# Projection back of a gated feed-forward block: one group of eleven pairs by seven products each, with quarter loads and adding loads

## The chip, the cores and the metric

The kernel runs on one core of a Trainium2 chip. The metric is the device time of one execution in microseconds (us). Engines: PE (TensorE, matrix products), DVE (VectorE), ACT (ScalarE), POOL (GpSimd), SP (SyncE, which issues most transfers). PEld is PE's weight loading. A transfer issued by POOL can add to what lies at its destination; here it is called an adding load.

## What is computed

One block of a hybrid sequence model over 1024 tokens of 1024 features, all in float32: a normalised projection into two branches (a chunkwise linear recurrence and a sparse attention), a gated mix of both and an output projection, and then the part that matters here, the feed-forward block with its final norm:

```python
h = h + mixed @ w_out[l]
f = rms_norm(h, g_norm_ffn[l])
h = h + (jax.nn.silu(f @ w_gate[l]) * (f @ w_up[l])) @ w_down[l]   # D_FF = 2816
return rms_norm(h, g_final)
```

The last product, (1024 x 2816) by (2816 x 1024), is called the projection back below.

## The kernel before

Each float32 operand is split into a rounded high part and a low rest (`split_steps`, L1868: ACT copies the high part at L1865, DVE subtracts it at L1862), and a product is three matmuls, high by high, high by low and low by high (`mm3`, L352 to L355). One matmul is 128x128 by 128x512.

Large products are saved by Strassen's scheme in Winograd's form: a product of 2 by 2 blocks takes seven block products and some sums instead of eight block products. The blocks of the output are token rows by parity (r) and column halves (c); the contraction is blocked in pairs. Of the 2816 hidden features, in 22 strips of 128 (`d_gu` in HBM, one strip per t), strips 2p and 2p+1 form **pair** p.

The projection back (L2487 to L2612) takes 9 of the 11 pairs by seven products, in two groups (`GROUPS`, 4 and 5 pairs). In a group, each product q runs over the pairs with four PSUM banks (one per token block j): 12 matmuls per pair. After each product DVE adds the four banks to accumulators in SBUF (`acc`), and behind the second group `combine(q)` adds accumulators to each other, on DVE or on POOL (`BOTH`). The sums of inputs that the products need are made by DVE (`into(SUM, ...)`), eight per pair. The remaining four strips (`tl`) are multiplied plainly, each of eight row blocks by two column halves by four strips, 12 matmuls each, and behind each row block its norm follows (`square`, `rstd_steps`, `stt`) and its rows go out. Inputs come as whole strips of 512 KB (`load2`), the residual `d_h` by plain loads into the accumulators.

The stages from the output projection on are recorded as steps (`Plan.step`) and put in order by a list planner (`Plan.run`, L139) with costs for each engine and a model of when a transfer lands (`landed`, `lat`). It sets the order on every engine and leaves none to run time. Transfers by SP are modelled with a size; adding loads (`dma_add`, L1874) only had a fixed latency, and SP's model did not know of them. Adding loads are used before in three places: `wo_add` (sums of blocks of w_out), `xadd` (the input x added to the output projection) and the second half of `sums` in the feed-forward products.

Ahead of the projection back run the feed-forward products up (`product`, L2311), which write `d_gu` at the end of every second strip; before these the output projection (`wprod`, products 1, 2, 6, 5, 3, 7, 4) and the norm behind it (`stored`, `rows_f`).

```python
def mm3(ps, ah, al, bh, bl, first, last):
    nc.tensor.matmul(ps, ah, bh, start=first, stop=False)   # L353
    nc.tensor.matmul(ps, ah, bl, start=False, stop=False)   # L354
    nc.tensor.matmul(ps, al, bh, start=False, stop=last)    # L355
```

Of the kernel before, what the change touches and what calls it, by code (L numbers as in the profile page):

```python
# [8 lines left out]
F32 = mybir.dt.float32  # L9
F32R = mybir.dt.float32r  # L10
AF = mybir.ActivationFunctionType
ALU = mybir.AluOpType
# [53 lines left out]
class Plan:  # L66
# [69 lines left out]
    def run(self):  # L136
        free = self.free_banks()
        while any(self.todo.values()):
# [26 lines left out]
            if st.nd:  # L165
                st.lat = self.landed[-1] - st.end
# [6 lines left out]
def body(ctx, tc, a, out):  # L173
# [1700 lines left out]
    def dma_add(dst, src, writes, lat):  # L1874
        pl.step((("Pool", 1000.0),), lambda e: nc.gpsimd.dma_start(dst(), src(), accum_op=ALU.add), (), writes, lat=lat)
# [614 lines left out]
    RSL = (0, 1, 2, 3, 28, 29, 4, 5, 16, 17, 18, 19, 8, 9, 10, 11, 30, 12, 13, 14, 15)  # L2490
    TMP, MORE, OUT = (12, 13, 14, 15), (6, 7, 4, 5), (3, 28, 29, 16)
    cnt = {"o": 0, "r": 0, "t": 0}

    def turn(kind, ring):
        cnt[kind] += 1
        return ring[(cnt[kind] - 1) % len(ring)]

    def load2(src, reads=()):

        n = turn("r", RSL)  # L2500
        bs = pieces(n)
        dma(lambda: slot_ap(n, F32), lambda: src.rearrange("p (a c) -> p a c", a=2), reads, bs, kb=512.0)
        return bs

    def op(src, n=None):
        b = slot_buf(turn("o", OPS) if n is None else n, F32R)
        split_steps(lambda: b.ap[:, 0, :], lambda: b.ap[:, 1, :], lambda: src.ap, [src], [b], V)
        return b

    allf = list(fsb.values())  # L2510
    acc = {}
    for n, q in enumerate((1, 2, 7, 5, 6, 4, 3, 8)):
        for j in range(4):
            z = 4 * n + j
            acc[q, j] = xpiece(z - 16) if z > 15 else pl.buf((), None, allf, make=lambda z=z: big(0, F32)[:, z, :])
    pl.boost = -100
    for q, r, c in ((2, 0, 0), (4, 1, 0), (8, 1, 1), (3, 0, 1)):
        for j in range(4):
            dma(lambda q=q, j=j: acc[q, j].ap, lambda r=r, c=c, j=j: d_h[2 * j + r][:, 512 * c:512 * c + 512],
                [hdr[2 * j + r]], [acc[q, j]], kb=512.0)  # L2520

    def combine(q):

        for j in range(4):
            g = lambda n: acc[n, j]
            todo = {2: ((2, 1),), 6: ((1, 6), (7, 1), (8, 5), (8, 7), (5, 1)), 4: ((4, 7),), 3: ((3, 5),)}.get(q, ())
            for d, x in todo:
                into(BOTH, g(d), g(d), g(x), ALU.add, [g(x)])

    pl.boost = 0  # L2530
    wdn = a["w_down"]
    for gi, pairs in enumerate(GROUPS):
        ra, rb = {}, {}
        for z in range(2):
            for p in pairs:
                t = 2 * p + z
                ra[p, z] = load2(d_gu[t][:, :], [gub[t]])
                rb[p, z] = load2(wdn[P * t:P * t + P, :])
        for q in QS:
            ps = [pl.buf() for _ in range(4)]  # L2540
            for p in pairs:
                (a11, a21), (a12, a22) = ra[p, 0], ra[p, 1]
                (b11, b12), (b21, b22) = rb[p, 0], rb[p, 1]
                if q == 7:
                    s3, t3 = piece(turn("t", TMP)), piece(turn("t", TMP))
                    into(SUM, s3, a11, a21, ALU.subtract, [a11, a21])
                    into(SUM, t3, b22, b12, ALU.subtract, [b22, b12])
                    x, y = s3, t3
                elif q == 5:
                    into(SUM, a21, a21, a22, ALU.add, [a22])  # L2550
                    into(SUM, b12, b12, b11, ALU.subtract, [b11])
                    x, y = a21, b12
                elif q == 6:
                    into(SUM, a11, a21, a11, ALU.subtract, [a21])
                    into(SUM, b11, b22, b12, ALU.subtract, [b22, b12])
                    x, y = a11, b11
                elif q == 4:
                    into(SUM, b21, b21, b11, ALU.subtract, [b11])
                    x, y = a22, b21
                elif q == 3:  # L2560
                    into(SUM, a12, a12, a11, ALU.subtract, [a11])
                    x, y = a12, b22
                else:
                    x, y = (a11, b11) if q == 1 else (a12, b21)
                oa, ob = op(x), op(y)

                def go(e, oa=oa, ob=ob, ps=ps, first=p == pairs[0], last=p == pairs[-1]):
                    for j in range(4):
                        js = slice(P * j, P * j + P)
                        mm3(ps[j].ap, oa.ap[:, 0, js], oa.ap[:, 1, js], ob.ap[:, 0, :], ob.ap[:, 1, :], first, last)  # L2570
                pl.step((("PE", 12 * 226.7),), go, [oa, ob], ps)
# [92 lines left out]
```

## Time and profile before

| | us |
|---|---|
| median of 3 runs | 1555.11 (1553.91 to 1556.33) |
| the profiled execution, device time | 1554.78 |
| its span, first to last instruction | 1553.0 |
| around the span | 1.8 |
| mean granted clock | 0.997 |

The span is that of one execution; the sum below is made against it, and the median of the runs lies 0.33 us above the profiled execution's own time. Times in rows count from the span's start. In a row of a timeline the first number is the start, the second the length, then engine, line, operation, out<-in, shapes and count, and in brackets how long the engine had been idle before and what ended that. Matmuls overlap: the row of one reads 0.39 us, while the next starts 0.23 us after it.

### The profile page before, as it was taken

Reading aid. Unit: us, or ns where it says so; the run is one execution under the profiler, and the core shown is the slowest. Engines: PE = TensorE matmul, PEld = TensorE weight load, DVE = VectorE, ACT = ScalarE, POOL = GpSimd, SP = SyncE. Lnnn points to the kernel's source line nnn. Section 1 sums busy time; section 2 is a strip of 40 time slices with the busy share of each in tenths; the row PEclk is TensorE's granted clock in tenths of the full one; section 3 lists DMA queues with packets and bytes.
Section 4 is the critical chain, followed back from the end, with each engine's and each line's share of the span. In section 5 each row is a group of like instructions: output and inputs, shape, how many; then the busy total and the mean of one; then the engine's idle time right before and its main releaser. Section 6 shows DMA issues by size and latency. Waiting matters only on the chain.

```text
span 1553.0 us, 22069 instructions
## 1 busy us (share of the span) xinstructions
PE 1516.0 (98%) x7642; PEld 1277.9 (82%) x7642; DVE 1174.5 (76%) x2464; ACT 803.4 (52%) x1708; POOL 194.4 (13%) x252
## 2 busy tenths in 40 slices
PE   6999999999999999999999999999999999999997
PEld 5877888887989888888887878888888888788876
DVE  6978888875988687865676795666666666988996
ACT  5325565653878688875434663333333333454433
POOL 2000000013121322110001510000000000001140
PEclk9999999999999999999999999999999999999999
DMA  8424755589242914239917825444454445560302
GB/s 276 121 76 127 232 162 170 162 239 269 42 114 40 186 39 115 48 81 345 259 41 176 177 75 129 110 110 113 117 168 109 109 109 183 190 217 1 109 1 108
DMA packets 185959, 211.84 MB, mean 136 GB/s; under 512 B 10536, under 2 KB 143046, under 8 KB 185848
## 3 DMA queue, kind: packets, MB, share of 16 engines
q1 hardware_dynamic: 153848, 179.91, 36.9%
q0 software_dynamic: 31712, 29.87, 12.8%
q8 instruction: 60, 0.98, 0.3%
q10 hardware_dynamic: 288, 0.66, 0.1%
q14 instruction: 51, 0.42, 0.1%
HBM read 159.97 MB, written 58.29 MB: 141 GB/s over the span
## 4 chain that ended last, share of the span: by engine, by line
PE 85%; DVE 6%; DMA 5%; ACT 2%; issue 1%; SPq 0%; POOL 0%; DVEq 0%; ACTq 0%; POOLq 0%
PE PS L354 16%; PE PS L355 16%; PE PS L353 16%; PE bk L353 5%; PE bk L354 5%; PE bk L355 5%; PE T L1526 4%; PE obank L1548 2%; PE obank L1546 2%; PE d L353 2%; PE d L355 2%; PE d L354 2%; DMA UTL_float<-in_x 1%; DMA rp<-in_w_in 1%; DMA d_mg<-S 1%
## 5 line engine op out<-in xcount | busy, mean ns | idle before, releaser
L1862 DVE TENSOR_TENSOR UTL_float<-PS,UTL_float 128x512 f32<-128x512 f32 x144 | 97.3, 689 | 80.2 <-PE PS L355 79.2
L1535 DVE TENSOR_TENSOR TL<-T,TH 128x512 fp32r<-128x512 f32 (+1 forms) x184 | 103.4, 582 | 28.7 <-ACT TH L1531 27.8
L1531 ACT ACTIVATE TH<-T 128x512 fp32r<-128x512 f32 (+1 forms) x184 | 90.3, 510 | 26.3 <-PE T L1526 23.1
L354 PE MATMUL PS<-quad_float32r,sl_float32r 128*128 128x512 f32 x240 | 93.4, 389 | 0.0
L353 PE MATMUL bk<-UTH,op 128*128 128x512 f32 x192 | 77.4, 403 | 0.0
L353 PE MATMUL PS<-quad_float32r 128*128 128x512 f32 x196 | 76.3, 389 | 0.0
L355 PE MATMUL PS<-quad_float32r 128*128 128x512 f32 x196 | 76.3, 389 | 0.0
L354 PE MATMUL PS<-quad_float32r 128*128 128x512 f32 x196 | 76.3, 389 | 0.0
L355 PE MATMUL bk<-UTH,op 128*128 128x512 f32 x192 | 75.0, 391 | 0.0
L354 PE MATMUL bk<-UTL,op 128*128 128x512 f32 x192 | 74.9, 390 | 0.0
L354 PE MATMUL PS<-quad_float32r,whi 128*128 128x512 f32 x176 | 68.6, 390 | 0.7 <-DVE quad_float32r L1862 0.7
L354 PE MATMUL PS<-quad_float32r,wh 128*128 128x512 f32 x164 | 63.8, 389 | 0.0
L353 PE MATMUL bk<-T,op 128*128 128x512 f32 x144 | 58.1, 404 | 0.0
L355 PE MATMUL bk<-T,op 128*128 128x512 f32 x144 | 56.3, 391 | 0.0
L354 PE MATMUL bk<-T,op 128*128 128x512 f32 x144 | 56.2, 390 | 0.0
L353 PE MATMUL d<-UTH,whi 128*128 128x512 f32 x128 | 53.1, 414 | 1.7 <-ACT mg L1398 1.5
L1865 ACT ACTIVATE quad_float32r<-quad_float 128x512 fp32r<-128x512 f32 x57 | 32.8, 622 | 41.3 <-PE PS L354 29.4
L1560 POOL DMA_DIRECT2D d_yn<-os x32 | 31.9, 996 | 173.9 <-DMA d_yn<-os 40.7
L354 PEld LDWEIGHTS PS<-quad_float32r,sl_float32r 128*128 128x128 f32 x240 | 45.1, 188 | 9.3
L355 PE MATMUL d<-UTH,wlo 128*128 128x512 f32 x128 | 50.4, 394 | 0.0
L354 PE MATMUL d<-UTL,whi 128*128 128x512 f32 x128 | 50.4, 393 | 0.0
L353 PE MATMUL PS<-UTH_float32r,sl_float32r 128*128 128x512 f32 x124 | 48.4, 390 | 0.0
(1488 smaller groups left out, 4933.9 us busy)
## 6 DMA issues: line engine op xcount, KB each, us to landing
rp<-in_w_in SPq DMA_DIRECT2D x22, 512.0 KB, 4.8
d_gu<-UTL_float SPq DMA_DIRECT2D x44, 256.0 KB, 3.2
sl_float<-in_w_up SPq DMA_DIRECT2D x20, 512.0 KB, 3.8
quad_float<-d_mg SPq DMA_DIRECT2D x32, 256.0 KB, 7.2
d_rep<-d_row SPq DMA_DIRECT2D x8, 960.0 KB, 7.4
quad_float<-d_gu SPq DMA_DIRECT2D x12, 512.0 KB, 6.1
quad_float<-in_w_down SPq DMA_DIRECT2D x12, 512.0 KB, 6.5
raw<-in_w_gate SPq DMA_DIRECT2D x11, 512.0 KB, 4.2
```

The costliest lines, as they stand in the source:

```text
L353: nc.tensor.matmul(ps, ah, bh, start=first, stop=False)
L354: nc.tensor.matmul(ps, ah, bl, start=False, stop=False)
L355: nc.tensor.matmul(ps, al, bh, start=False, stop=last)
L1526: nc.tensor.transpose(pt[:, z, P * r:P * r + P], e, ident)
L1531: nc.scalar.activation(hl[0][:, 0:m], pt[:, 0:m], AF.Copy)
L1535: nc.vector.tensor_tensor(hl[1][:, 0:m], pt[:, 0:m], cast32(hl[0])[:, 0:m], ALU.subtract)
L1546: nc.tensor.matmul(po, vv, th[:, z, :], start=(st[1] == 0), stop=False)
L1548: nc.tensor.matmul(po, vv, tl[:, z, :], start=False, stop=(st[1] == st[2]))
L1560: low_half.append(lambda: nc.gpsimd.dma_start(dst, half(1), accum_op=ALU.add))
L1862: return pl.step(alts, lambda e: ENG[e].tensor_tensor(out_(), x(), y(), alu), reads, writes, **kw)
L1865: return pl.step((("ACT", cost),), lambda e: nc.scalar.activation(out_(), x(), fn), reads, writes, **kw)
```

## The change

The projection back becomes one group of all 11 pairs by seven products. The four strips that were multiplied plainly are gone. Inputs are loaded by quarters of a pair (128x512, 256 KB; `load`, `gu`, `wd`). Of the sums of inputs, those of `w_down` are made by adding loads on POOL (`more`), those of `d_gu` by DVE, four per pair (`into(V, a3...)` and three `neg_sum`). A product ends in four banks that are copied by ACT or combined by DVE into four blocks of four pieces (`v1`, `v7`, `w4`, `c22`); `acc` and `combine` are gone. The residual is added by 16 adding loads from `d_h`. In the last product the first six pairs run over all four token blocks, the last five block by block, and each block's norm follows it. The ring of split operands (`OPS`) grows from 12 to 14 slots, seven pairs. In the final norm, the first column half of seven of the eight row blocks is scaled by ACT and multiplied by the gain on POOL (the `two` form of `stt`); before this was so for both halves of one row block.

The planner now knows the size of adding loads and lets them and SP's transfers share one model of landing. With this it also orders a few steps of the output projection and the feed-forward products differently.

```diff
-                st.lat = self.landed[-1] - st.end
+                st.lat = max(st.lat, self.landed[-1] - st.end)
...
-    def dma_add(dst, src, writes, lat):
-        pl.step((("Pool", 1000.0),), lambda e: nc.gpsimd.dma_start(dst(), src(), accum_op=ALU.add), (), writes, lat=lat)
+    def dma_add(dst, src, writes, lat, reads=(), kb=256.0):
+        pl.step((("Pool", 1000.0),), lambda e: nc.gpsimd.dma_start(dst(), src(), accum_op=ALU.add), reads, writes, lat=lat, kb=kb, nd=1)
...
-        dma_add(lambda: b.ap, lambda: wo_blk(kh, ch), [b], 12000.0)
+        dma_add(lambda: b.ap, lambda: wo_blk(kh, ch), [b], 12000.0, kb=1024.0)
...
-    GROUPS = ((0, 1, 2, 3), (4, 5, 6, 7, 8))
-    QS = (1, 2, 7, 5, 6, 4, 3)
-    OPS = (20, 21, 22, 23, 24, 25, 26, 27, 31, 33, 32, 34)
...
-    tl = range(2 * (GROUPS[-1][-1] + 1), NFF)
...
+    NPR = NFF // 2
+    OPS = (20, 21, 22, 23, 24, 25, 26, 27, 31, 33, 32, 34, 6, 7)
+    cnt = [0]
+    allf = list(fsb.values())
+    room = [(n, z) for n in (0, 1, 2, 3, 28, 29, 4, 5, 30, 8, 9, 10, 11, 16, 17, 18, 19, 14, 15, 12, 13) for z in range(2)]
+    room += [("u", n) for n in range(16)]
...
+    def more(b, src, reads=()):
+        dma_add(lambda: b.ap, lambda: src, [b], 5500.0, reads)
+
+    def mult(ps, js, ops, first, last):
+        def go(e):
+            for j in js:
+                for n, (oa, ob) in enumerate(ops):
+                    cs = slice(P * j, P * j + P)
+                    mm3(ps[j].ap, oa.ap[:, 0, cs], oa.ap[:, 1, cs], ob.ap[:, 0, :], ob.ap[:, 1, :], first and n == 0, last and n == len(ops) - 1)
+        pl.step((("PE", 3 * 226.7 * len(js) * len(ops)),), go, [b for o in ops for b in o], [ps[j] for j in js])
+
+    def product(xs, ys):
+        ps = [pl.buf() for _ in range(4)]
+        for p in range(NPR):
+            mult(ps, range(4), [(op(xs[p]), op(ys[p]))], p == 0, p == NPR - 1)
+        return ps
...
+    for p in PR:
+        a1[p] = gu(0, 0, p)
+        xx[p] = load(wd(0, 0, p))
+    ps = product(a1, xx)
+    for j in J:
+        act(587.0, at(v1[j]), at(ps[j]), AF.Copy, [ps[j]], [v1[j]])
+    a3, yy = {}, {}
+    for p in PR:
+        a3[p] = gu(0, 1, p)
+        yy[p] = load(wd(0, 1, p))
+        more(yy[p], wd(1, 1, p))
+        more(xx[p], wd(0, 1, p))
+        into(V, a3[p], a1[p], a3[p], ALU.subtract, [a1[p]])
+    ps = product(a3, yy)
...
+    for p in PR:
+        a4[p] = gu(1, 1, p)
+        neg_sum(a3[p], a3[p], a4[p])
+        neg_sum(a1[p], a3[p], a1[p])
+    ps = product(a1, xx)
+    for j in J:
+        into(V, w4[j], ps[j], v1[j], ALU.add, [ps[j], v1[j]])
+    give(*a1.values())
+    for p in PR:
+        more(xx[p], wd(1, 1, p))
+    ps = product(a3, xx)
+    for j in J:
+        neg_sum(w4[j], ps[j], w4[j])
+        into(V, c22[j], w4[j], v7[j], ALU.subtract, [w4[j], v7[j]])
+        into(V, v7[j], ps[j], v7[j], ALU.add, [ps[j]])
+        into(V, v7[j], v7[j], v1[j], ALU.add, [v1[j]])
+    for p in PR:
+        more(xx[p], wd(1, 0, p))
+    ps = product(a4, xx)
...
+    for r, c, b in ((1, 0, v7), (1, 1, c22), (0, 0, v1), (0, 1, w4)):
+        for j in J:
+            more(b[j], *row(r, c, j))
...
+    ps = product(a2, zz)
+    give(*zz.values())
+    normal(1, (0, 1), (v7, c22))
+    normal(1, (2, 3), (v7, c22))
...
+    for p in range(6):
+        mult(ps, J, [(op(a2[p]), op(bb[p]))], p == 0, False)
+    tail = [(op(a2[p]), op(bb[p])) for p in range(6, NPR)]
+    for j in J:
+        mult(ps, [j], tail, False, True)
+        into(V, w4[j], w4[j], ps[j], ALU.subtract, [ps[j]])
+        square(at(w4[j]), 2 * j, 1, [w4[j]])
+        normal(0, (j,), (v1, w4))
```

Three places of the order of instructions. The first is ACT in the output projection, where product 5's operands are split (`sl_5` and `sl_7` are its left operand's high parts, `sl_14` and `sl_12` its right operand's; `sq,sml` is the sum of squares of a row block that waits for an adding load of x). This is one piece of the difference:

```order
 L1865 ACTIVATE wl_7547<-ra_7544 128x512
-L2097 ACTIVATE sq,sml<-UTL_float_8419 128x512
 L1865 ACTIVATE sl_5_float32r<-UTH_float_7797 128x512 x2
 L1865 ACTIVATE sl_7_float32r<-UTH_float_7797 128x512 x2
 L2097 ACTIVATE sq,sml<-UTL_float_8419 128x512
-L1865 ACTIVATE sl_14_float32r<-quad_2_float_7569 128x512 x2
-L1865 ACTIVATE sl_12_float32r<-quad_2_float_7569 128x512
+L1865 ACTIVATE sl_14_float32r<-quad_2_float_7569 128x512
 L2097 ACTIVATE sq,sml<-UTL_float_8419 128x512
```

The left operand's four splits now stand ahead of the first sum of squares and no longer wait for its load; the right operand's still stand behind it.

The second is DVE at the end of the second group before, behind product 4 (`UTH` and `UTL` are accumulators; `whi`, `wlo`, `wh`, `wl` are the split operands of product 3's first pairs):

```order
L1862 TENSOR_TENSOR UTL_float_8419<-UTL_float_8419,PS 128x512 x4
L1862 TENSOR_TENSOR UTH_float_11728<-UTH_float_11728 128x512
L1862 TENSOR_TENSOR UTH_float_11728<-UTH_float_11728,UTL_float_8419 128x512
L1862 TENSOR_TENSOR UTL_float_8419<-UTL_float_8419,UTH_float_11728 128x512
L1862 TENSOR_TENSOR UTH_float_11728<-UTH_float_11728 128x512 x2
L1862 TENSOR_TENSOR UTL_float_8419<-UTL_float_8419,UTH_float_11728 128x512 x2
L1862 TENSOR_TENSOR whi_7018<-ra_7544,whi_7018 128x512
L1862 TENSOR_TENSOR wlo_7019<-sl_20_float_9298,wlo_7019 128x512
```

and what stands in its place now, behind the fourth product (`UTL` holds the pieces v1, v7, w4, c22; `quad_20` on the left and `sl` are operands of the fifth product's later pairs):

```order
L2039 SCALAR_TENSOR_TENSOR UTL_float_8419<-PS,UTL_float_8419 128x512 x2
L1862 TENSOR_TENSOR UTL_float_8419<-UTL_float_8419 128x512 x2
L1862 TENSOR_TENSOR UTL_float_8419<-PS,UTL_float_8419 128x512 x2
...
L1862 TENSOR_TENSOR quad_20_float32r<-UTH_float_11928,quad_20_float32r 128x512
L1862 TENSOR_TENSOR quad_20_float32r<-sl_20_float_9298,quad_20_float32r 128x512
```

The 16 sums behind the fourth product stand in one block, ahead of the splits of the fifth product's later pairs; the sums of accumulators that stood ahead of product 3's first pairs are gone.

The third is POOL from the last feed-forward weight on. Before:

```order
L1875 DMA UTL_float_8419<-in_w_up 128x4x128
L1862 TENSOR_TENSOR UTH_float_11728<-UTH_float_11728 128x512 x3
L1862 TENSOR_TENSOR UTL_float_8419<-UTL_float_8419,UTH_float_11728 128x512 x3
L1862 TENSOR_TENSOR UTH_float_11728<-UTH_float_11728,UTL_float_8419 128x512 x2
...
L1862 TENSOR_TENSOR sl_20_float_9072<-sl_20_float_9072,sl_20_float_9068 128x512 x2
```

Now (60 adding loads and seven multiplications; `sl`, `raw`, `ra` at the start are the w_down quarters `xx`, `quad_20_float_11632` and `11701` the quarters `yy`; `d_h` is the residual):

```order
L1875 DMA sl_20_float_8957<-in_w_down 128x512
L1875 DMA quad_20_float_11632<-in_w_down 128x512
L1875 DMA sl_20_float_9000<-in_w_down 128x512
L1875 DMA quad_20_float_11632<-in_w_down 128x512
L1875 DMA sl_20_float_9068<-in_w_down 128x512
L1875 DMA sl_20_float_9072<-in_w_down 128x512
L1875 DMA quad_20_float_11701<-in_w_down 128x512
...
L1875 DMA UTL_float_8419<-d_h_152 128x512
...
L1862 TENSOR_TENSOR UTH_float_11928<-UTH_float_11928 128x512 x3
```

The 20 additions of accumulators are gone from POOL; each adding load of an `xx` stands in a queue with those of `yy`, in the order of the pairs.

## Rows read from the trace of the kernel before

**Rows 1.** The page, part 1 (busy time, share of the span, instructions) and the first line of part 4 (the chain that ended last, by engine).

```profile
PE 1516.0 (98%) x7642; PEld 1277.9 (82%) x7642; DVE 1174.5 (76%) x2464; ACT 803.4 (52%) x1708; POOL 194.4 (13%) x252
...
PE 85%; DVE 6%; DMA 5%; ACT 2%; issue 1%; SPq 0%; POOL 0%; DVEq 0%; ACTq 0%; POOLq 0%
```

**Rows 2.** Timeline of PE in the projection back: its first matmul (1324.88), the 61st matmul (1338.48) and the one behind it, the first two matmuls of product 3 of the second group, the end of the slow stretch behind them, and the last matmul.

```profile
1324.88 0.39 PE L353 MATMUL PS<-quad_float32r 128*128 128x512 f32 x1
...
1338.48 0.40 PE L353 MATMUL PS<-wl,wh 128*128 128x512 f32 x1
1339.81 0.50 PE L354 MATMUL PS<-wl,wh 128*128 128x512 f32 x1 [0.94 <-DVE wl L1862]
...
1483.92 0.39 PE L353 MATMUL PS<-wlo,whi 128*128 128x512 f32 x1
1486.42 0.80 PE L354 MATMUL PS<-wlo,whi 128*128 128x512 f32 x1 [2.12 <-DVE wlo L1862]
...
1490.11 0.39 PE L354 MATMUL PS<-wlo,whi 128*128 128x512 f32 x1
...
1544.76 0.39 PE L355 MATMUL PS<-quad_float32r,sl_float32r 128*128 128x512 f32 x1
```

**Rows 3.** Busy time by stretch: stretch, its length, busy us (and instructions) of PE, PEld, DVE, ACT, POOL, granted clock of PE, busy share of the DMA engines, GB/s. The first is in the output projection, the others in the projection back.

```profile
840.00:860.00 20.00, 18.34 (x79) 14.28 (x78) 19.07 (x32) 17.27 (x36) 4.81 (x5) 1.00 0.60 130
...
1324.88:1340.00 15.12, 14.18 (x63) 11.45 (x62) 12.02 (x20) 9.52 (x18) 0.00 (x0) 1.00 1.03 395
1340.00:1483.00 143.00, 143.00 (x631) 118.35 (x631) 133.43 (x203) 67.40 (x117) 19.46 (x13) 1.00 0.26 92
1480.00:1490.00 10.00, 7.88 (x29) 6.07 (x28) 10.00 (x13) 3.02 (x6) 4.46 (x3) 0.83 0.00 0
1490.00:1545.00 55.00, 55.00 (x244) 45.30 (x242) 45.35 (x104) 20.88 (x51) 9.82 (x8) 1.00 0.16 58
```

**Rows 4.** Timeline of DVE ahead of the two waits of PE (rows 2): the split that ended the first, and the sums and splits ahead of the second.

```profile
1339.08 0.68 DVE L1862 TENSOR_TENSOR wl<-quad_float,wl 128x512 fp32r<-128x512 f32 x1
...
1478.31 3.48 DVE L1862 TENSOR_TENSOR UTH_float<-UTH_float 128x512 f32<-128x512 f32 x2
1481.70 3.46 DVE L1862 TENSOR_TENSOR UTL_float<-UTL_float,UTH_float 128x512 f32<-128x512 f32 x2
1485.09 0.68 DVE L1862 TENSOR_TENSOR whi<-ra,whi 128x512 fp32r<-128x512 f32 x1
1485.69 0.68 DVE L1862 TENSOR_TENSOR wlo<-sl_float,wlo 128x512 fp32r<-128x512 f32 x1
...
1488.10 3.08 DVE L1862 TENSOR_TENSOR quad_float32r<-quad_float,quad_float32r 128x512 fp32r<-128x512 f32 x5
```

**Rows 5.** Timeline of POOL in the same stretch: the additions of accumulators.

```profile
1479.50 1.73 POOL L1862 TENSOR_TENSOR UTH_float<-UTH_float,UTL_float 128x512 f32<-128x512 f32 x1
1481.31 1.62 POOL L1862 TENSOR_TENSOR UTH_float<-UTH_float 128x512 f32<-128x512 f32 x1
1483.01 1.61 POOL L1862 TENSOR_TENSOR UTL_float<-UTL_float,UTH_float 128x512 f32<-128x512 f32 x1
```

**Rows 6.** Timeline of ACT in the output projection: the sum of squares that waits for an adding load of x, and the splits of product 5's operands behind it.

```profile
839.55 0.63 ACT L2097 ACTIVATE sq<-UTL_float 128x512 bf16<-128x512 f32 x1 [6.86 <-DMA UTL_float<-in_x]
...
840.19 2.18 ACT L1865 ACTIVATE sl_float32r<-UTH_float 128x512 fp32r<-128x512 f32 x4
...
842.88 1.65 ACT L1865 ACTIVATE sl_float32r<-quad_float 128x512 fp32r<-128x512 f32 x3
```

**Rows 7.** Timeline of PE there: the first matmuls of product 5.

```profile
843.55 0.50 PE L353 MATMUL PS<-sl_float32r,sl_float32r 128*128 128x512 f32 x1 [0.98 <-ACT sl_float32r L1865]
844.59 0.50 PE L354 MATMUL PS<-sl_float32r,sl_float32r 128*128 128x512 f32 x1 [0.54 <-DVE sl_float32r L1862]
```

**Rows 8.** The line of the adding loads: their length on POOL (min/median/max ns) for a piece of 128x512, and the time from issue to landing of all its adding loads.

```profile
L1875 POOL DMA_DIRECT2D UTL_float<-in_x x16: 850/867/1421, 824.6 to 868.6; - x16
...
DMA to landing us min/median/max: 4.0/6.9/17.0
```

**Rows 9.** Timeline of POOL in the output projection: two adding loads issued back to back.

```profile
865.69 1.82 POOL L1875 DMA_DIRECT2D UTL_float<-in_x  x2 [0.90 <-DVE UTL_float L1862]
```

**Rows 10.** Timeline of DVE in the same two microseconds: subtractions with both inputs in SBUF.

```profile
865.31 1.89 DVE L1862 TENSOR_TENSOR quad_float32r<-quad_float,quad_float32r 128x512 fp32r<-128x512 f32 x3
```

**Rows 11.** DMA queue of the adding loads in the stretch 700 to 900 us: packets, MB, share of that stretch's 200 us of 16 engines.

```profile
q0 software_dynamic: 4944, 9.44, 26.7%
```

**Rows 12.** DMA issues from 1300 us on: out<-in, count, KB each, median us from issue to landing.

```profile
quad_float<-d_gu SPq DMA_DIRECT2D x12, 512.0 KB, 6.1
...
d_gu<-UTL_float SPq DMA_DIRECT2D x4, 256.0 KB, 7.2
```

**Rows 13.** Timeline of SP: the write of the next-to-last piece of `d_gu`.

```profile
1326.81 0.32 SPq L1872 DMA_DIRECT2D d_gu<-UTL_float  x1
```

**Rows 14.** Timeline of DVE behind the last matmul: the last sum, and the last scaling.

```profile
1545.26 0.69 DVE L1862 TENSOR_TENSOR UTL_float<-UTL_float,PS 128x512 f32<-128x512 f32 x1 [1.82 <-PE PS L355]
...
1549.05 0.74 DVE L2127 SCALAR_TENSOR_TENSOR raw<-UTL_float,sml,sl_float 128x512 f32<-128x512 f32 x1
```

More of the change, by code (lines that the diff above doesn't have):

```diff
@@ L2505, in op, with take @@
[L2505 to L2506 removed]
+    NPR = NFF // 2
[4 more added lines that the diff above has]
+    room += [("u", n) for n in range(16)]
+    def take():
+        h = room.pop(0)
+        b = pl.buf([("V", h[1])], None, allf, make=lambda: big(0, F32)[:, h[1], :]) if h[0] == "u" else fpiece(*h)
+        b.home = h
+        return b
@@ L2507, in op, with give, load @@
+    def give(*bs):
+        for b in bs:
+            room.append(b.home)
+    def load(src, reads=()):
+        b = take()
+        dma(lambda: b.ap, lambda: src, reads, [b])
+        return b
+    def op(src):
+        b = slot_buf(OPS[cnt[0] % len(OPS)], F32R)
+        cnt[0] += 1
         split_steps(lambda: b.ap[:, 0, :], lambda: b.ap[:, 1, :], lambda: src.ap, [src], [b], V)
         return b
[L2510 to L2515, printed above, removed]
@@ L2530, in body @@
-    pl.boost = 0
-    wdn = a["w_down"]
[L2532 to L2571, printed above, removed]
-            for j in range(4):
-                d = acc[q, j]
-                if gi == 0 and q not in (2, 3, 4):
-                    act(480.0, lambda d=d: d.ap, lambda s=ps[j]: s.ap, AF.Copy, [ps[j]], [d])
-                else:
-                    ew(V, lambda d=d: d.ap, lambda d=d: d.ap, lambda s=ps[j]: s.ap, ALU.add, [ps[j]], [d])
-            if gi == len(GROUPS) - 1:
-                combine(q)
@@ new lines, in normal @@
+                dma(lambda i=i, c=c: out[P * i:P * i + P, 512 * c:512 * c + 512], lambda o=o: o.ap, [o])
+                give(o)
+    J = range(4)
+    PR = range(NPR)
+    v1, v7, w4, c22 = ([xpiece(4 * n + j) for j in J] for n in range(4))
+    at = lambda b: (lambda: b.ap)
+    a1, xx = {}, {}
+    for p in PR:
[5 more added lines that the diff above has]
+    a3, yy = {}, {}
@@ new lines, in body @@
+    for r, c, b in ((1, 0, v7), (1, 1, c22), (0, 0, v1), (0, 1, w4)):
+        for j in J:
+            more(b[j], *row(r, c, j))
+    gl = [load(a["g_final"][512 * c:512 * c + 512].partition_broadcast(P)) for c in range(2)]
+    for j in J:
+        square(at(c22[j]), 2 * j + 1, 1, [c22[j]])
+        into(V, v7[j], ps[j], v7[j], ALU.add, [ps[j]])
+        square(at(v7[j]), 2 * j + 1, 0, [v7[j]])
+    a2, zz = {}, {}
+    for p in PR:
+        a2[p] = gu(1, 0, p)
+        zz[p] = load(wd(1, 0, p))
@@ new lines, in body @@
+    ps = product(a2, zz)
+    give(*zz.values())
+    normal(1, (0, 1), (v7, c22))
+    normal(1, (2, 3), (v7, c22))
+    for j in J:
+        into(V, v1[j], ps[j], v1[j], ALU.add, [ps[j]])
+        square(at(v1[j]), 2 * j, 0, [v1[j]])
+    bb = {}
+    for p in PR:
+        bb[p] = load(wd(1, 1, p))
+        neg_sum(a2[p], a3[p], a2[p])
+    ps = [pl.buf() for _ in J]
+    for p in range(6):
+        mult(ps, J, [(op(a2[p]), op(bb[p]))], p == 0, False)
+    tail = [(op(a2[p]), op(bb[p])) for p in range(6, NPR)]
```

69 lines of the change are left out of this document (21 added, 48 removed).

## Prediction, made before the changed kernel ran

> **What bounds the kernel now.** I read the page's shares first: PE is busy 98% of the span and carries 85% of the chain that ended last, while DVE is at 76% [rows 1]. So what the change is worth is read on PE: how many matmuls it issues, and where it waits. The timeline of PE gives both for the projection back, which begins at 1324.88 and issues its last matmul at 1544.76 [rows 2]. From 1324.88 to 1338.48 there are 60 steps, so a step is 13.60 / 60 = 0.2267 us. The code counts 948 matmuls: 7 products x 9 pairs x 12 = 756, and 16 blocks x 12 = 192. At 0.2267 that is 214.9 us; the stretch takes 1544.76 + 0.23 - 1324.88 = 220.1. PE thus loses 5.2 us here, and the timeline shows where. One wait at 1339.81: the step from 1338.48 is 1.33 us instead of 0.23, 1.1 lost. One at 1486.42: 2.50 instead of 0.23, 2.27 lost, and behind it nine steps to 1490.11 take 3.69 us instead of 2.04, 1.65 lost; the stretch by time shows a granted clock of 0.83 there [rows 3]. Together 5.0 of the 5.2.
>
> Both waits end on a DVE split. The stretches show why: from 1340 to 1483 DVE is busy 133.4 of 143 us [rows 3], and ahead of the second wait four sums of accumulators take 1.7 us each (3.48 and 3.46 for two) where five splits in a row take 3.08, that is 0.6 each [rows 4]. In the same microseconds POOL adds accumulators [rows 5].
>
> **The change, part by part.**
>
> *Matmuls.* 7 x 11 x 12 = 924, 24 fewer. PE has no other work there, so each is worth a step: 24 x 0.2267 = **-5.4 us**.
>
> *DVE's load.* A split or sum costs 0.6 [rows 4]. Before, seven products of nine pairs have 126 splits of the low part and 72 sums of inputs, then 16 splits, 56 sums out of PSUM (40 on DVE here, 16 on ACT), 32 sums of accumulators shared with POOL, and 16 last sums. Now: 154 splits, 44 sums of inputs, 32 sums at the ends of products. By product, in a window of 11 x 12 x 0.2267 = 29.9 us, DVE has 33 operations in the second (20 us), 22 + 22 in the third (26.6), 22 + 4 in the fourth, 22 + 16 in the fifth (23), and under 27 us in each of the last two, norms included. None fills its window, and the ring lets splits run up to seven pairs, 19 us, ahead. The two places that cost PE time, the first sums of product 7 beside its splits and the sums of accumulators beside POOL, are gone. I take both waits and the slow steps behind the second as gone: **-5.0 us**; the bounds are 0 (a wait of equal size elsewhere) and -5.2.
>
> *The 16 sums behind the fourth product* stand in front of later splits on DVE. They take 16 x 0.6 to 0.7, some 10 us from the first finished bank, about 2 us before the product's end. The split of the fifth product's seventh pair behind them is then done about 10 us after that end, and needed 6 x 2.72 = 16.3 us after it. Cover 6 us, cost 0.
>
> *POOL's queue.* An adding load of this size occupies POOL for 0.87 us and lands after 6.9 (4.0 to 17.0) [rows 8]. Each `xx` quarter is read by one product's split and needed by the next product's: one window, 29.9 us, later. The load needs at most 0.9 + 17.0 + 1.2 for the new split, so 10 us are left. Eleven issues take 10 us of a window. Cost 0, but this is the part with the least room (first rival).
>
> *SP's queue.* The last pair's `d_gu` quarter can be read back only when its strip is written. That write goes out at 1326.81 [rows 13] and takes 7.2, the load some 6.1 [rows 12], both splits 1.3: 1341.4; PE wants it at 1324.88 + 10 x 2.72 = 1352.1. Queued behind it on SP are the second product's quarters from the sixth pair on: the sixth is loaded by about 1341, has its adding load by 1351 and its splits by 1353, and is due at 1354.8 + 13.6 = 1368.4. Cost 0.
>
> *Output projection.* There ACT waited 6.86 us for an adding load of x in front of a sum of squares, with eight splits of product 5 queued behind [rows 6]; PE then waited 0.98 and 0.54 on these splits [rows 7], 1.66 us idle in that stretch [rows 3]. Now four of the splits stand ahead of that wait and the rest between sums of squares. The right operand's first high part would be out at about 840.8 instead of 843.4. Bounds: 0 (the later sums wait as long) and -1.7; I take **-1.2**, nearer the full size, since PE needs the first half of the splits first.
>
> *POOL's seven multiplications* of the final norm. The trace prices them: a DVE sum of two SBUF inputs beside POOL's additions took 1.7 instead of 0.6 [rows 4, 5], so each costs DVE up to 1.1 us. Four run in the last two products' windows, 4.4 us that fit; three near the end beside sums that read PSUM, like the sum of 0.69 at the end [rows 14]. The Trainium skill, page "SBUF — State Buffer", section "Who interferes with whom", says that a DVE instruction with two SBUF inputs contends with a GpSimd instruction that reads SBUF, and not with one that only writes it. The trace agrees with the first half (1.7 us against 0.6); by the second half the adding loads would cost DVE nothing.
>
> *Tail.* From the last sum to the span's end: 1553.0 - 1545.26 = 7.7 us [rows 14]. The last block's chain is the same (sum, square, norm, two scalings on DVE, two stores). Cost 0; 0.5 either way.
>
> **Sum.** 1554.78 - 5.4 - 5.0 - 1.2 = 1543.2 for the profiled execution; the median of the runs lies 0.33 above it: **1543.5 us**.
>
> **Rivals.**
>
> *1. Adding loads fill the DMA engines.* In 700 to 900 us their queue took 26.7% of 200 us for 9.44 MB [rows 11], 5.7 us per MB; plain loads run at 395 GB/s when full [rows 3], 2.5 us per MB. Until the second product's end (1385), from about 1308 on, 36 quarters (9.4 MB, 24 us) and 22 adding loads (5.8 MB, 33 us) must pass: 57 of 72 us to the last split. If adding loads run half as slow again, 73 us, and the second product's last pairs come some 2 us late, then the same once more in the third: 4 to 6 us, as large as the waits that went. 1548.5. For it: the DMA share was 1.03 in the first stretch [rows 3]. Against it: that was 512 KB loads in a burst, and the first pairs' quarters are now fetched long before.
>
> *2. Slower: POOL's issues hold DVE up.* If an adding load's issue blocked DVE as POOL's additions do (1.1 us each), then the second product's window would hold 20 + 22 x 1.1 = 44 us of DVE work in 29.9, the third 26.6 + 12 = 39, the fifth 23 + 16 x 1.1 = 41: 34 us too much, 1577. The point from which it eats the whole gain of 11.6 is 0.65 us per issue (49 issues, less the 20 us of room in these three windows). Against it: beside two issues of POOL three DVE subtractions took 1.89 us, 0.6 each [rows 9, 10].
>
> *3. POOL's issues wait for DVE.* Where DVE leaves a tenth of the time, as in the third window (26.6 of 29.9), an issue that could only run in DVE's pauses would take 0.87 / 0.11 = 8 us, eleven of them 87 us instead of 29.9, and PE would wait near 57 us: 1600. Against it: the two issues beside a full DVE took 1.82 us, 0.9 each [rows 9, 10]. The Trainium skill has such a rule on the page "SBUF — State Buffer", section "SBUF: two separate sides": a DMA from the GpSimd queue starves for descriptors while DVE runs in a 2-port mode. By that rule this change would lose; the trace shows no such wait with these float32 sums.
>
> *4. No change.* The waits move (rival 1 in full, some 5 us), the output projection gains nothing, and the last block by block stretch leaves DVE late by its norm chain of 3.4 to 3.9 us per block where PE takes 15 x 0.2267 = 3.4: up to 3 us at the end. 1543.5 + 5 + 1.2 + 3 = 1552.7.
>
> **Chances.** The forecast (1541 to 1546) 0.72; rival 1 (1546 to 1551) 0.17; rival 4 0.05; rival 2 0.04; rival 3 0.02. A difference under 0.2%, 3.1 us, can't be told from none. So faster 0.72 + 0.17 = 0.89, same 0.05, slower 0.06. The range for 8 in 10 runs from 1540.5 (all bounds at their good end, and half a microsecond of the tail) to 1549.5 (well into rival 1).
>
> **What would show it.** Right: 24 fewer matmuls; PE from the first to the last matmul of the projection back in about 209.5 us with steps of 0.2267 and a granted clock of 1.00; no wait of PE on a split; DVE under 0.9 busy; POOL's issues 0.87 each and DVE's splits 0.6 beside them; product 5 of the output projection with less than 0.5 us of wait. Wrong: waits of PE at the start of the second or third product with DVE waiting for a transfer (rival 1), DVE operations over 1 us beside issues (rival 2), issues over 1 us (rival 3), or a last sum later than 0.5 us behind the last matmul (rival 4).

## The result, and the profile after

| | before | after |
|---|---|---|
| median of the runs compared | 1554.51 (4 runs, 1553.69 to 1556.33) | 1544.32 (4 runs, 1542.82 to 1546.87) |
| the profiled execution / its span | 1554.78 / 1553.0 | 1544.09 / 1542.3 |

The changed kernel takes 0.9935 of the time before (95% interval 0.9917 to 0.9952): about 10 us faster, beyond the 0.2% that can be told from none. The median lies 0.8 us above the forecast. Where the 10.7 us between the two spans went is read on PE.

The page after, part 1 and the first line of part 4 [rows 1]:

```profile
PE 1507.2 (98%) x7618; PEld 1271.8 (82%) x7618; DVE 1130.6 (73%) x2393; ACT 807.6 (52%) x1715; POOL 225.0 (15%) x297
...
PE 85%; DVE 6%; DMA 6%; ACT 2%; issue 1%; SPq 0%; DVEq 0%; ACTq 0%; POOLq 0%
```

24 matmuls fewer are listed. Timeline of PE: the first matmul of product 5 of the output projection and the one wait left there [rows 7], then the first and the last matmul of the projection back [rows 2]:

```profile
842.36 0.39 PE L353 MATMUL PS<-sl_float32r,sl_float32r 128*128 128x512 f32 x1
...
844.30 0.50 PE L354 MATMUL PS<-sl_float32r,sl_float32r 128*128 128x512 f32 x1 [0.17 <-DVE sl_float32r L1862]
...
1323.54 0.39 PE L353 MATMUL PS<-quad_float32r 128*128 128x512 f32 x1
...
1532.75 0.39 PE L355 MATMUL PS<-sl_float32r,sl_float32r 128*128 128x512 f32 x1
```

From 1323.54 to 1532.75 + 0.23 are 209.44 us, which is 924 x 0.22667: no wait and no slow step is left in this stage. Before it was 220.1, so 10.7 went here. The stage also begins 1.34 earlier. What lies behind the last matmul grew: 1542.3 - 1532.98 = 9.3, where it was 1553.0 - 1544.99 = 8.0. Sum: -10.7 - 1.3 + 1.3 = -10.7.

The stretches of the projection back after, columns as in [rows 3]:

```profile
1323.54:1355.00 31.46, 31.46 (x140) 26.08 (x139) 21.36 (x34) 14.66 (x25) 11.49 (x14) 1.00 1.10 273
1355.00:1385.00 30.00, 30.00 (x134) 24.82 (x134) 26.41 (x44) 15.74 (x28) 5.00 (x6) 1.00 0.97 306
1385.00:1415.00 30.00, 30.00 (x134) 24.86 (x133) 18.79 (x31) 12.92 (x23) 12.04 (x14) 1.00 0.99 208
...
1475.00:1505.00 30.00, 30.00 (x134) 24.86 (x133) 28.04 (x51) 19.25 (x38) 6.51 (x4) 1.00 0.19 71
```

PE fills every stretch at a granted clock of 1.00. The DMA engines are full or nearly so for 90 us (the last two columns: their share, 0.97 to 1.10, and GB/s). Their transfers from 1326 to 1345, by queue and by issue:

```profile
q0 software_dynamic: 1160, 2.11, 60.2%
q1 hardware_dynamic: 1801, 3.28, 49.6%
...
quad_float<-d_gu SPq DMA_DIRECT2D x6, 256.0 KB, 15.6
quad_float<-in_w_down POOLq DMA_DIRECT2D x6, 256.0 KB, 14.3
```

The adding loads (q0) hold the engines 0.602 x 19 / 2.11 = 5.4 us per MB, the plain ones 2.9, and a quarter lands 15.6 us after its issue where `d_gu` took 6.1 [rows 12]. Yet PE waits for none.

Behind the fourth product, DVE's block of sums and POOL's adding loads beside it:

```profile
1442.35 1.28 DVE L2039 SCALAR_TENSOR_TENSOR UTL_float<-PS,UTL_float 128x512 f32<-128x512 f32 x2
1443.55 1.28 DVE L1862 TENSOR_TENSOR UTL_float<-UTL_float 128x512 f32<-128x512 f32 x2
...
1450.75 1.28 DVE L1862 TENSOR_TENSOR UTL_float<-UTL_float 128x512 f32<-128x512 f32 x2
1451.95 0.68 DVE L1862 TENSOR_TENSOR quad_float32r<-UTH_float,quad_float32r 128x512 fp32r<-128x512 f32 x1
```

```profile
1444.53 7.07 POOL L1875 DMA_DIRECT2D UTL_float<-d_h  x8 [17.26 <-DVE UTL_float L1862]
```

Sums with two SBUF inputs keep to 0.6 us beside eight issues of 0.88; beside POOL's additions they took 1.7 [rows 4, 5]. At the end, DVE and POOL behind the last products:

```profile
1530.39 0.74 DVE L2127 SCALAR_TENSOR_TENSOR quad_float<-UTL_float,sml,UTH_float 128x512 f32<-128x512 f32 x1
1531.32 0.98 DVE L2106 TENSOR_TENSOR sml<-sml 128x1 f32<-128x1 f32 x1 [0.19 <-ACT sq L2097]
...
1533.61 0.69 DVE L1862 TENSOR_TENSOR UTL_float<-UTL_float,PS 128x512 f32<-128x512 f32 x1
...
1535.14 0.95 DVE L2106 TENSOR_TENSOR sml<-sml 128x1 f32<-128x1 f32 x1 [0.19 <-ACT sq L2097]
1536.13 0.15 DVE L2107 TENSOR_SCALAR sml<-sml 128x1 f32<-128x1 f32 x1
```

```profile
1526.91 1.29 POOL L1862 TENSOR_TENSOR sl_float<-sl_float,UTH_float 128x512 f32<-128x512 f32 x1 [34.50 <-ACT sl_float L2123]
1530.69 1.59 POOL L1862 TENSOR_TENSOR quad_float<-quad_float,UTH_float 128x512 f32<-128x512 f32 x1 [2.49 <-ACT quad_float L2123]
1534.52 1.56 POOL L1862 TENSOR_TENSOR quad_float<-quad_float,UTH_float 128x512 f32<-128x512 f32 x1 [2.24 <-ACT quad_float L2123]
```

The norm's first tiny sum, 128x1, takes 0.98 and 0.95 us where its neighbours take 0.15, and it ends when POOL's multiplication ends: 1532.30 and 1532.28, 1536.09 and 1536.08. The other way round, DVE's scaling of 1530.39, which also has two SBUF inputs but started before POOL's multiplication, keeps the 0.74 of [rows 14], and that multiplication takes 1.59 where the one of 1526.91 took 1.29. The first of the two slow sums also makes the last sum of a product late: that starts 0.63 behind the last matmul's end, not the 0.27 of [rows 2, 14].

### The profile page after: what moved, and what is told of

The parts are those of the page before. It is cut to its first block, busy times and chain, and to the rows that moved or that the text cites. A ratio compares the mean times of both kernels' runs of the same rounds, so it can differ in the third digit from the quotient of the medians.

```text
span 1542.3 us, 22142 instructions
## 1 busy us (share of the span) xinstructions
PE 1507.2 (98%) x7618; PEld 1271.8 (82%) x7618; DVE 1130.6 (73%) x2393; ACT 807.6 (52%) x1715; POOL 225.0 (15%) x297
## 4 chain that ended last, share of the span: by engine, by line
PE 85%; DVE 6%; DMA 6%; ACT 2%; issue 1%; SPq 0%; DVEq 0%; ACTq 0%; POOLq 0%
PE PS L354 16%; PE PS L353 16%; PE PS L355 16%; PE bk L353 5%; PE bk L354 5%; PE bk L355 5%; PE T L1526 4%; PE obank L1548 2%; PE obank L1546 2%; PE d L353 2%; PE d L355 2%; PE d L354 2%; DMA UTL_float<-in_x 1%; DMA d_mg<-S 1%; DMA ra<-in_w_gate 1%
## 5 line engine op out<-in xcount | busy, mean ns | idle before, releaser
L1862 DVE TENSOR_TENSOR UTL_float<-PS,UTL_float 128x512 f32<-128x512 f32 x160 | 107.5, 688 | 85.2 <-PE PS L355 84.1
L354 PE MATMUL PS<-quad_float32r,sl_float32r 128*128 128x512 f32 x216 | 84.0, 389 | 0.0
L353 PE MATMUL PS<-quad_float32r 128*128 128x512 f32 x192 | 74.8, 390 | 0.0
L355 PE MATMUL PS<-quad_float32r 128*128 128x512 f32 x192 | 74.7, 389 | 0.0
L354 PE MATMUL PS<-quad_float32r 128*128 128x512 f32 x192 | 74.7, 389 | 0.0
L354 PE MATMUL PS<-quad_float32r,whi 128*128 128x512 f32 x168 | 65.5, 390 | 0.7 <-DVE quad_float32r L1862 0.7
L353 PE MATMUL PS<-UTH_float32r,sl_float32r 128*128 128x512 f32 x124 | 48.4, 391 | 0.0
L355 PE MATMUL PS<-UTH_float32r,sl_float32r 128*128 128x512 f32 x124 | 48.3, 389 | 0.0
L725 ACT ACTIVATE op<-S 128x512 fp32r<-128x512 f32 x40 | 25.1, 629 | 43.6 <-PE bk L354 35.0
```

The source lines that it names most:

```text
L725: step1("ACT", 525.0, lambda: nc.scalar.activation(h, src(), AF.Copy), [r], [b])
L1862: return pl.step(alts, lambda e: ENG[e].tensor_tensor(out_(), x(), y(), alu), reads, writes, **kw)
```

## Experiments

They ran on three chips, each beside the kernel before. "Stage" is from the first to the last matmul of the projection back, "end" what lies behind it, both of the profiled execution.

**The changed kernel again.**

> The changed kernel unchanged, as the measure for the other runs of this chip. Theory and rivals alike: 1544.3 us within 1.5, and the same stretches as in its first profile: from the first to the last matmul of the projection back 209.4 us, behind the last matmul 9.3.

Measured: 1545.3 us, 0.9933 of before (0.9919 to 0.9947); stage 209.44, end 9.3. But the stage began at 1324.72, 1.2 us later than in the first profile. What delayed it stands ahead of the feed-forward products, on PE:

```profile
893.34 0.72 PE L353 MATMUL PS<-UTH_float32r,whi 128*128 128x512 f32 x1 [1.11 <-ACT UTH_float32r L1865]
894.55 0.79 PE L354 MATMUL PS<-quad_float32r,whi 128*128 128x512 f32 x1 [0.49 <-DVE quad_float32r L1862]
895.14 0.63 PE L355 MATMUL PS<-UTH_float32r,whi 128*128 128x512 f32 x1
```

Behind three short waits, eleven matmuls go at a granted clock of 0.50 (the stretch from 895 to 899), which is 1.2 of 2.4 GHz: 0.43 us from one to the next, against 0.23, 2.2 us in all; this execution had reached the place 1.3 us earlier than the first profile (893.34 instead of 894.61). Over all 14 profiled executions here there were no such steps at this place in four and 5 to 11 in ten, with the old and with the new order, and the stage began between 1322.3 and 1325.9.

**Only the planner's model, in the kernel before, and the changed kernel without it.** In the first the transfer model alone is new:

```diff
-                st.lat = self.landed[-1] - st.end
+                st.lat = max(st.lat, self.landed[-1] - st.end)
...
+        pl.step(..., reads, writes, lat=lat, kb=kb, nd=1)
```

> The kernel before with the planner's new landing model of adding loads alone; the projection back is the old one. Theory (the output projection's gain of 1.3 us comes from this model alone, through the new order of ACT): PE's waits of 0.98 and 0.54 us at the start of product 5 go, the projection back starts near 1323.5 instead of 1324.9, and the time is 1.3 us less than that of the kernel before, about 1553.2. Rival (the gain belongs to something else in the change): the waits stay and the time is that of the kernel before within 0.3 us in the place where the projection back starts.

Measured: 0.9994 of before (0.9984 to 1.0003), 1554.62 us. Both waits went: product 5 began at 842.34 without one. The stage began at 1324.26, 0.6 earlier, since seven slow steps gave back 1.4.

In the second, `nd=1` is kept for the adding loads of the projection back alone:

> The changed kernel with the planner's old model for the three old uses of adding loads; the new projection back keeps the new model. Theory: the output projection takes its old order again, product 5 waits some 1.5 us again, the projection back starts near 1324.9 and then runs its 209.4 us without a wait; 1.3 us more than the changed kernel, about 1545.6. Rival: no place where PE waits comes back, 1544.3; or the projection back gains waits too because its start is ordered differently, 1547 or more.

Measured: 1545.71 us, 0.9938 of before (0.9926 to 0.9951), beside 0.9933 of the changed kernel. The waits came back, 1.09 and 0.54; the stage began at 1324.53 and took 209.44. So the model moves the splits and takes the two waits away, as forecast, and in the old projection back it gives nothing more (the stage took 220.2). What it does for the order of the new projection back was not tested, since this run keeps it there. Its worth in the whole time isn't resolved: the half clock behind it takes some or all of it in part of the executions. The stage began at 1325.1 in the mean of the three profiled executions with the old order, at 1324.0 in that of the eleven with the new one, and single executions of either differ by more than that.

**The norm's tiny sum with one input as a scalar operand.**

```diff
+            if len(rows) == 1:
+                nc.vector.tensor_scalar(at(2), at(0), at(1), 1.0 / D, ALU.add, ALU.mult)
+                nc.vector.tensor_scalar(at(2), at(2), 1.0, EPS, ALU.mult, ALU.add)
+                return
```

> The changed kernel with the tiny sum of the final norm (128x1, two inputs in SBUF) written as a tensor_scalar with one input as a scalar operand, wherever a norm covers one row block. Theory (the two tiny sums at the end take 0.95 and 0.98 us instead of 0.16 because they read two SBUF inputs while POOL multiplies): they take 0.2 each, the end behind the last matmul becomes 8.0 to 8.5 us instead of 9.3, and the time about 1543.4. Rival 1 (the scalar operand contends with POOL as well): 0.9 us each again, 1544.3. Rival 2 (the end is set by the last sum, which starts late, or by the store, not by the tiny sum): the sum gets short and the end stays at 9.3.

Measured: 1543.73 us, 0.9929 of before (0.9917 to 0.9942). On DVE:

```profile
1532.22 0.21 DVE L2107 TENSOR_SCALAR sml<-sml 128x1 f32<-128x1 f32 x1 [0.19 <-ACT sq L2097]
...
1533.97 0.69 DVE L1862 TENSOR_TENSOR UTL_float<-UTL_float,PS 128x512 f32<-128x512 f32 x1
...
1535.51 0.21 DVE L2107 TENSOR_SCALAR sml<-sml 128x1 f32<-128x1 f32 x1 [0.19 <-ACT sq L2097]
```

0.21 instead of 0.95, both in the midst of a POOL multiplication (1531.60 to 1533.18 and 1534.66 to 1536.44), the last sum 0.19 behind the last matmul's end (1533.78), the end 8.1 instead of 9.3. The trace shows the 1.2 us at their place; between whole runs they lie inside the intervals.

**The last three multiplications on DVE instead of POOL.**

```diff
-... c == 0 and i != 6)
+... c == 0 and r == 1)
```

> The changed kernel with the last product's three multiplications on DVE instead of POOL. Theory (POOL's three multiplications cost the end 0.8 us through the tiny sum that they slow, but save DVE three scalings of 0.67): the tiny sums take 0.16 us again, DVE's last sum starts right behind the last matmul, but two scalings of the block before now stand ahead of the last norm; the end is 9.3 to 9.8 us, the time as the changed kernel's or 0.4 us more. Rival (POOL's multiplications are a loss as a whole): the end falls to 8.0 to 8.5, the time by about 1 us.

Measured: 1545.52 us, 0.9942 (0.9927 to 0.9957); tiny sums of 0.16, the end 9.5. Giving POOL the multiplications is neither a gain nor a loss; what cost was the form of the sum beside them.

**The kernel before with all sums of accumulators on DVE.**

```diff
-                into(BOTH, g(d), g(d), g(x), ALU.add, [g(x)])
+                into(V, g(d), g(d), g(x), ALU.add, [g(x)])
```

> The kernel before with the 32 sums of accumulators all on DVE, none on POOL. Theory (POOL's additions beside DVE's, which took 1.7 us each instead of 0.6, made the second wait): behind product 4 of the second group 16 sums of 0.6, 9.6 us, stand where 7 sums took 11.6; its split is done some 1.4 us earlier, the wait of 2.27 us at 1486 falls to about 1, the slow clock behind it may go, and the time is 1.4 to 3.9 us under the kernel before, 1551.5 to 1554. Rival (DVE has too much to do there, whatever POOL does): 20 more sums are 12 us more for DVE in two products, PE waits at other splits, and the time is that of before or up to 3 us more, 1555 to 1558.

Measured: 1.0006 of before (0.9997 to 1.0014). The sums took 0.6 each, the first split behind them came at 1483.05 instead of 1485.09, and PE still waited, twice, without slow steps:

```profile
1484.39 0.50 PE L354 MATMUL PS<-quad_float32r 128*128 128x512 f32 x1 [1.81 <-DVE quad_float32r L1862]
1494.01 0.50 PE L355 MATMUL PS<-quad_float32r 128*128 128x512 f32 x1 [0.94 <-DVE quad_float32r L1862]
```

The stage took 219.5 instead of 220.1. The theory falls: POOL's contention cost DVE about what POOL took off it. The sums were enough for a wait by themselves. They stand behind product 6 and not, as the orders ahead of the prediction have it, behind product 4. In the kernel before, DVE adds product 6's banks, then the sums of accumulators follow, and product 4's banks come only behind them:

```profile
1471.07 2.47 DVE L1862 TENSOR_TENSOR UTL_float<-UTL_float,PS 128x512 f32<-128x512 f32 x4
1473.46 1.53 DVE L1862 TENSOR_TENSOR UTH_float<-UTH_float 128x512 f32<-128x512 f32 x1
...
1491.11 2.46 DVE L1862 TENSOR_TENSOR UTL_float<-UTL_float,PS 128x512 f32<-128x512 f32 x4
```

**The changed kernel with 16 sums more behind its fourth product.**

```diff
+        for alu in (ALU.add, ALU.subtract) * 2:
+            into(V, w4[j], w4[j], v1[j], alu, [v1[j], ps[j]])
         neg_sum(w4[j], ps[j], w4[j])
```

> The changed kernel with 16 sums more on DVE behind the fourth product (each w4 block has v1 added and subtracted twice; nothing else changes but rounding). No additions on POOL stand beside them. Theory (the old second wait was the amount of DVE work behind a product, and the cover there is now some 6.3 us: the split behind the block is done at 1453.2 and its pair due at 1459.5): 9.6 us more eat the cover, PE waits 3.0 to 3.6 us in the fifth product, slow clock for up to 1.7 us more; 1547 to 1550. Rival (DVE's work alone makes no wait, it needed POOL beside it): no wait, 1544 to 1545.

Measured: 1551.09 us, 0.9962 of before (0.995 to 0.9974). DVE's block ran from 1443.90 to 1463.12 at 0.6 a sum, and PE:

```profile
1464.47 0.79 PE L354 MATMUL PS<-quad_float32r 128*128 128x512 f32 x1 [3.00 <-DVE quad_float32r L1862]
1465.06 0.63 PE L355 MATMUL PS<-quad_float32r 128*128 128x512 f32 x1
```

```profile
1465.00:1470.00 5.00, 5.00 (x13) 3.87 (x12) 5.00 (x10) 1.97 (x6) 2.67 (x4) 0.50 1.12 226
```

A wait of 3.0 and 13 slow steps behind it, at a granted clock of 0.50 (the stretch from 1465): the stage took 215.6, 6.1 more. DVE's sums alone bring such a wait back, of the size that the cover of 6.3 us says (9.6 - 6.3 = 3.3). The time lies above the 1550 that I had allowed, mainly because the slow steps cost 2.6 us, not 1.7. One of the six executions took 1546.75.

**The w_down sums on DVE, by plain loads, instead of adding loads.**

```diff
     def more(b, src, reads=()):
-        dma_add(lambda: b.ap, lambda: src, [b], 5500.0, reads)
+        if reads:
+            dma_add(lambda: b.ap, lambda: src, [b], 5500.0, reads)
+            return
+        t = load(src)
+        into(V, b, b, t, ALU.add, [t])
+        give(t)
```

> The changed kernel with the w_down sums made by plain loads and additions on DVE instead of adding loads (the residual is still added by adding loads). Theory (the adding loads are what keeps DVE under its window): the second product has 33 + 22 operations of 0.6 us on DVE, 33 us in 29.9, the third 44 + 11, also 33 where it was 26.6; with seven pairs of lead some of it is caught, PE waits 3 to 8 us there in sum, 1548 to 1553. Rival (the ring's lead of 19 us takes all of it, and the adding loads were not needed): no wait, 1545.

Measured: 1543.6 us, 0.9931 of before (0.9916 to 0.9947), stage 209.45: no wait. The stretches:

```profile
1325.00:1355.00 30.00, 30.00 (x134) 24.86 (x133) 29.01 (x49) 14.77 (x26) 0.00 (x0) 1.00 1.04 376
1355.00:1385.00 30.00, 30.00 (x135) 24.82 (x134) 30.00 (x51) 14.64 (x26) 0.00 (x0) 1.00 0.59 193
1385.00:1415.00 30.00, 30.00 (x134) 24.86 (x133) 27.30 (x46) 12.70 (x22) 0.00 (x0) 1.00 0.65 207
```

My theory is refuted: DVE is busy for 30 of 30 us and PE doesn't wait. As I read it, the sums aren't urgent and run ahead of the product that needs them: DVE has 49 operations in the first of these stretches where the changed kernel has 34, and most of that stretch lies ahead of the second product. The adding loads gain nothing that shows here. What they cost shows beside it: the same bytes as plain loads moved at 376 GB/s instead of 273, and the quarters landed 5.3 us after their issue instead of 15.6.

**A ring of 12 slots**, in the changed kernel and in the one with the sums on DVE:

```diff
-    OPS = (20, 21, 22, 23, 24, 25, 26, 27, 31, 33, 32, 34, 6, 7)
+    OPS = (20, 21, 22, 23, 24, 25, 26, 27, 31, 33, 32, 34)
```

> The changed kernel with a ring of 12 slots for split operands, as before, instead of 14. Theory (one pair less of lead, 2.7 us, and the cover behind the fourth product falls from 6.3 to 3.6 us): no wait, 1544 to 1545.5. Rival (the longer ring is what took the waits away): waits of 1 to 3 us behind the fourth product or at the start of the second, 1546 to 1549.

Measured: 1545.72 us, 0.9934 (0.9918 to 0.9951), stage 209.45, no wait.

> Both: w_down sums on DVE and a ring of 12 slots. With the sums on DVE and 14 slots DVE was busy 29.0, 30.0 and 27.3 us of the 30 us stretches from 1325 to 1415 without a wait of PE. Theory (there the long ring and the early start carry it, so one pair less shows): PE waits 1 to 4 us between 1340 and 1400, 1546 to 1549. Rival (room is left even so): no wait, 1545.

Measured: 1544.31 us, 0.9921 (0.9907 to 0.9936), stage 209.5, no wait, against my theory of 1 to 4 us. So neither the longer ring nor the adding loads, nor both, took the waits away.

**Each adding load of the second product's operand twice.**

```diff
         more(yy[p], wd(1, 1, p))
+        more(yy[p], wd(1, 1, p))
```

> The changed kernel with each adding load into a quarter of the second product's right operand issued twice (that operand then holds one half of its sum twice): 11 adding loads more, between 1325 and 1370. Theory (the DMA engines are full there, and the last of these loads is some 9 us ahead of the matmul that needs it): 11 loads of 0.26 MB at the 1.5 to 2 us that one then takes are 16 to 22 us, 7 to 13 more than the lead; PE waits at the end of the second product and the time is 1551 to 1557. Rival (the engines have room, their share of 1.0 is not a limit): POOL's issues take 0.86 us each, 9.5 us more, just the lead; no wait, or one under 1 us, 1544 to 1546.

Measured: 1559.79 us, 1.0027 of before (1.0017 to 1.0038), more than either theory gave. PE waited, but in the first product:

```profile
1362.05 0.79 PE L353 MATMUL PS<-quad_float32r 128*128 128x512 f32 x1 [9.63 <-ACT quad_float32r L1865]
...
1396.37 0.50 PE L354 MATMUL PS<-quad_float32r 128*128 128x512 f32 x1 [0.97 <-DVE quad_float32r L1862]
```

ACT shows why:

```profile
1352.82 0.63 ACT L1865 ACTIVATE sl_float32r<-quad_float 128x512 fp32r<-128x512 f32 x1 [8.12 <-DMA quad_float<-in_w_down]
```

ACT's order has splits of the second product's operands ahead of the split of the first product's last pair. When those wait for an adding load, that one waits behind them. POOL idled up to 5.1 us for the first of two loads to land before it issued the second, so this run mixes the engines' load with the two in a row; which of them cost how much stays open.

**Sums on DVE and the tiny sum's form together.**

> Two edits that gained or cost nothing by themselves, together: the w_down sums on DVE by plain loads and additions, and the tiny sum of the norm with one input as a scalar operand. Theory (both act in different places): no wait of PE in the projection back, 209.4 us from its first to its last matmul, tiny sums of 0.2 us, 8.0 to 8.3 us behind the last matmul; 1.1 us less than the changed kernel, about 1543.3. Rival (the sums on DVE shift the order at the end and the gain of the tiny sum is lost): 9 us or more behind the last matmul, 1544.5.

Measured: 1543.67 us, 0.9918 of before (0.9904 to 0.9933), the lowest ratio of all; stage 209.44, end 8.0. The stage began at 1324.68 behind seven slow steps. It beats the kernel before; that it beats the changed one is shown by the end, 8.0 against 9.3, not by the whole times, whose intervals overlap.

## Why the prediction was right, and where it was off

- **Matmuls, -5.4:** right to the hundredth: the stage is 924 steps of 0.22667.
- **Waits, -5.0:** -5.2. Both waits and the slow steps went, and none took their place. My reason was half right. Sums of accumulators at 1.7 us were part of the second wait, but without POOL the wait stayed. It is the block of sums that DVE has behind a product, against the time until the next split is due. Before, that block ran from 1471.07 to 1485.09, and the splits behind it were due from 1483.92 on, one product of 13.6 us after product 6's end; now it takes 9.6 us and the split behind it is due 16.3 us after the end of its product. The change made the block shorter and the due time later at once; only the sums were varied alone, and 16 more brought the wait back. The first wait's own cause was not tested apart.
- **DVE's load:** "None fills its window" held but for one stretch (28.0 of 30 from 1475, over the 0.9 that I named). As a condition it was not needed: with the sums on DVE two windows were full and cost nothing.
- **The 16 sums, cover 6 us:** 6.3 by the trace (split done at 1453.2, due at 1459.5), and the run with 16 more waited as that says.
- **SP's and POOL's queues, 0:** the cost was 0, the cover much smaller than written. The last `d_gu` quarter was to be split at 1341.4, 10.7 us early; it took 15.6 us to land instead of 6.1, and its split ended on DVE near 1347.9 where PE needed it at 1350.7: 2.9 us left. The 6.9 us that I gave for the landing of an adding load of this size was the median of all sizes [rows 8]; the sixteen of this size had 8.8, and beside full DMA engines it became 14.3. Rival 1 was right that adding loads fill the engines (5.4 us per MB measured, 5.7 written), and wrong only in that PE felt it.
- **Rivals 2 and 3:** refuted by DVE's sums at 0.6 beside POOL's issues, and by the issues at 0.86 in the median. In 19 of the 60 a row reads over 1 us, up to 1.9, which I had named as the sign of rival 3; but those rows overlap, and twelve issues in a row from 1444.53 took 10.7 us, 0.9 each. The Trainium skill, page "SBUF — State Buffer", section "SBUF: two separate sides", ties the starving of such transfers to a 2-port mode of DVE. That the change would lose by this rule, as I wrote, took DVE's sums to run in such a mode, for which I had no row; no run here shows any starving beside them.
- **Output projection, -1.2:** -1.34 in the profile, the two waits gone but for 0.17. That the number came out so close is luck: the start of the stage differs by up to 2.8 us between executions with the new order, and what a run keeps depends on the half clock behind the norm, up to 2.2 us.
- **The step that failed: POOL's multiplications and the tail, 0 each.** The end grew by 1.3. I had priced a DVE sum of two SBUF inputs beside POOL at 1.1 us more, and then counted only the large operations near the end, which read PSUM. The norm's tiny sum also has two SBUF inputs: it took 0.8 us more in each of the last two blocks. About 0.8 falls on the last block's chain, and about 0.4 comes through the last sum, late behind the block before. This was the small form of rival 4's "norm chain", and its sign, a last sum later than 0.5 us behind the last matmul, came true with 0.63: the tiny sums of the last two blocks lie 3.8 us apart where PE takes 3.4 for a block. What I had missed in the trace is that the price isn't set by the size of DVE's operation: the tiny sum stood until POOL's instruction was through. The Trainium skill, page "SBUF — State Buffer", section "SBUF: two separate sides", says just that: whichever of the two starts first has the shared ports for its whole instruction. The trace agrees, to 0.02 us, and in the other direction too: DVE's scaling that started first kept its 0.74, and POOL's multiplication took 1.59 instead of 1.29. With a scalar operand in place of the second input the sum took 0.21.

The sum was 1543.2 for the profiled execution; it took 1544.09. The end's 1.3 makes up the difference, less some tenths that the waits and the output projection gave more, so the errors had opposite signs and part of the closeness is chance.

## What to carry to other kernels

A wait on an operand split was set here by the block of work that stands ahead of it in the engine's order, against the time until it is due; an engine's share of busy time over a window says little. When POOL starts to read SBUF beside DVE, list every DVE instruction with two SBUF inputs on the path: a tiny one waits too, until POOL's instruction is through, and a scalar operand freed it here. Loads that add held the DMA engines about twice as long per byte here (5.4 against 2.9 us per MB): look at the landing times of the plain loads beside them, which is where their cost appears first.

## What the runs showed that I had not expected

- A 128x1 sum of two SBUF inputs took 0.95 to 0.98 us beside a POOL multiplication, 0.15 to 0.16 without one, 0.21 with one input as scalar operand.
- Where PE waited three times within 4 us (2.3 to 2.7 us in all), the granted clock fell to half for no matmul or for 5 to 11, differently in executions of one kernel: up to 2.2 us. This is only part of what one execution's start of the stage differs from another's: without these steps the starts with the new order would still lie between 1321.2 and 1323.5.
- With adding loads among them the full DMA engines moved 273 GB/s, with plain loads alone 376, and plain quarters landed after 15.6 us instead of 5.3.
